# A one-core decoder block: borders of phases in another order, all splits on VectorE, state space steps further apart, and pre-norm gains in the weights' rows

## The chip, the cores and the metric

The kernel runs on one core of a Trainium2 chip, as one launch. The metric is the device time of that launch in microseconds (us). TensorE does the matrix products, ScalarE (ACT in the profile), VectorE (DVE) and GpSimd (POOL) work beside it, and SyncE (SP) issues most of the loads.

## The reference

256 tokens of 2048 channels, float32 throughout, run through five blocks, each with its norms, and a closing gate:

```python
def first_block(x, ...):                     # two layers
    h = x
    for layer in range(2):
        u = rms_norm(h, mix_norm_pre[layer])
        u = even_mixer(u, ...) if layer == 0 else odd_mixer(u, ...)
        h = h + rms_norm(u, mix_norm_post[layer])
        u = swiglu(rms_norm(h, ffn_norm_pre[layer]), w_gate, w_up, w_down)
        h = h + rms_norm(u, ffn_norm_post[layer])
    return h

def second_block(x, p, ...):
    hn = rmsnorm(h, norm_gain[i]); proj = hn @ w_in[i]
    ya = pool_mixer(...) * silu(pool_gate)
    yb = ssm_mixer(...) * silu(ssm_gate)     # a complex diagonal state space, 64 groups of 16 channels
    h = h + concatenate([ya, yb]) @ w_out[i]
    h = h + (p[i] @ w_ple[i]) * sigmoid(h @ w_ple_gate[i])
    return rmsnorm(h, final_gain)
```

The even mixer is stick-breaking attention and a gated delta rule, the odd one is block attention and dilated attention. A norm is `x * rsqrt(mean(x*x) + eps) * gain`; the gain of a pre-norm is one number per channel, so it may multiply either the normed activations or the rows of the matrix behind them.

## The kernel before

**Units and parts.** Every product with a large matrix is cut into units: 128 rows of the matrix by 512 columns. For float32 accuracy each operand is split in a high and a low piece (`uh`, `ul` of the activations, `wh`, `wl` of the weights), and a unit is three matmuls for each of the two token tiles (t = 0, 1, of 128 tokens): `wh`·`uh` (L300), `wl`·`uh` (L301), `wh`·`ul` (L302). Two units share one chunk of 512 KB, loaded by SyncE into a `wr` tile (L213, five buffers). `split()` (L219) makes a part of a chunk: ScalarE copies `wr` to `wh` (L227), VectorE subtracts to `wl` (L228). Parts are split SA = 3 ahead of the unit at hand, loads run LA = 4 chunks ahead. There are four own buffers for `wh` and `wl`; up to EXTRA more parts may stand in general tiles while `lead[0]` is set, and then GpSimd takes every other subtraction.

**Phases and borders.** The program has the phases mix0, ffn0, mix1, ffn1, blk2 and a last one (`ple` gate and final norm). `order()` (L234) lays out each phase's units: the first 12 (head) run for t=0 and then again for t=1, the middle ones for both, the last 8 (tail) for t=0 and then t=1. So the chain between two phases, in which a token tile's sum of squares, its root, the update of `h`, the transposes of `h` and the split into `uh` and `ul` follow each other, can run for one token tile while TensorE works for the other. Hooks in `order()` say ahead of which unit a step is emitted: T(t, c) transposes four blocks of `h` of tile t, columns 512c and on (L351), and evacuates them to `uh` (ScalarE, L358) and `ul` (VectorE, L360), with the pre-norm gain `gT` as the scale; U(t, c) is `upd` (L415), the update of `h` (VectorE L419 for c < 3; for c = 3 ScalarE L421 and GpSimd L422). T(t, c) has the activations of units 4c to 4c+3. After the last panel of a phase, `post_end` (L409) computes the root (GpSimd, L318).

**Tasks.** Attention, delta rule and state space are generators that `tick()` steps once per unit; `yield n` lets n units pass. `ssm_prep` (L1016) makes the tables of the state space during ffn0: its loop has 16 turns, each of which computes `cpo` (VectorE, L1244), sends it off and multiplies it on TensorE (L1249). `ssm_states` (L1356), in blk2, loads `csn`, multiplies the windows (L1371), has the result evacuated to `vt` by ScalarE (L1375 to L1379), transposes `vt` (L448), runs VectorE's scans into `vw` (L1389), and multiplies by `swap` (L1394).

All engines run their instructions in the order of emission; the program is scheduled by hand, and no planner moves anything.

## Time and profile before

| | |
|---|---|
| median of the three runs | 2908.78 us (2908.42 to 2912.8) |
| the profiled execution | 2910.4 us |
| its span | 2908.4 us |
| TensorE busy | 2826.9 us, 97% |
| VectorE / ScalarE / GpSimd busy | 58% / 47% / 9% |
| mean granted TensorE clock | 0.994 |

The span is the time from the first to the last instruction in the trace. TensorE's busy time is nearly all of it, so the views worth reading are those that say where it was not busy: the list of waits, and the timeline around them. PEclk is the share of full clock that TensorE was granted in a stretch.

### The profile page before, as it was taken

What the parts mean: (1) busy time and instruction counts of PE and PEld (TensorE: products, weight loads), DVE (VectorE), ACT (ScalarE), POOL (GpSimd) and SP (SyncE); (2) the same over time, 40 slices, a digit from 0 to 9 for tenths busy, and PEclk for the clock granted to TensorE, in tenths of its full rate; (3) what the DMA queues carried; (4) which work ended last, traced back from release to release, by engine and by line L of the source; (5) the groups of instructions that cost most, each with busy time, mean ns of one, the idle gap of its engine ahead of it and who ended that gap; (6) DMA issues with size and microseconds to landing.
All of it is one profiled execution on the core that took longest, in us unless ns stands there. A gap on an engine that the chain in (4) does not pass through costs nothing. (4 is left out here: it accounts for less than half of the span.)

```text
span 2908.4 us, 35734 instructions
## 1 busy us (share of the span) xinstructions
PE 2826.9 (97%) x13503; PEld 2314.7 (80%) x13503; DVE 1676.7 (58%) x2170; ACT 1357.4 (47%) x1876; POOL 258.1 (9%) x316
## 2 busy tenths in 40 slices
PE   8999999999999999989999999999999999999998
PEld 6877778778888778877888878888888887778887
DVE  5675555677665665565555564544544556464555
ACT  5554454544444434445444454444444445444444
POOL 1141510100000111020000010000000002100010
PEclk9999999999999999999999999999999999999999
DMA  7664645576767667645556656666666665875554
GB/s 229 179 166 126 179 151 175 165 200 201 221 210 214 202 201 252 202 153 173 172 167 181 189 164 189 188 192 192 188 190 194 189 200 167 290 232 179 188 192 153
DMA packets 303613, 552.17 MB, mean 190 GB/s; under 512 B 43032, under 2 KB 48720, under 8 KB 303440
## 3 DMA queue, kind: packets, MB, share of 16 engines
q1 hardware_dynamic: 293216, 515.53, 58.5%
q0 software_dynamic: 10224, 34.35, 3.7%
q8 instruction: 106, 1.74, 0.2%
q14 instruction: 67, 0.55, 0.1%
HBM read 532.24 MB, written 21.76 MB: 190 GB/s over the span
## 5 line engine op out<-in xcount | busy, mean ns | idle before, releaser
L228 DVE TENSOR_TENSOR wl<-wr,wh 128x1024 fp32r<-128x1024 f32 x930 | 1144.4, 1233 | 1040.7 <-ACT wh L227 1037.7
L227 ACT ACTIVATE wh<-wr 128x1024 fp32r<-128x1024 f32 x948 | 1000.5, 1059 | 1053.0 <-PE mm L302 1000.7
L300 PE MATMUL mm<-wh,uh 128*128 128x512 f32 x2624 | 1055.2, 402 | 2.9 <-ACT wh L227 2.2
L302 PE MATMUL mm<-wh,ul 128*128 128x512 f32 x2624 | 1028.4, 392 | 11.6 <-DVE ul L360 11.6
L301 PE MATMUL mm<-wl,uh 128*128 128x512 f32 x2624 | 1026.4, 391 | 4.3 <-DVE wl L228 4.3
L302 PEld LDWEIGHTS mm<-wh,ul 128*128 128x128 f32 x2624 | 494.2, 188 | 122.1 <-DVE ul L360 17.0
L300 PEld LDWEIGHTS mm<-wh,uh 128*128 128x128 f32 x2624 | 495.5, 189 | 104.5 <-ACT wh L227 4.2
L301 PEld LDWEIGHTS mm<-wl,uh 128*128 128x128 f32 x2624 | 495.8, 189 | 102.7 <-DVE wl L228 7.3
L300 PE MATMUL mm<-wh,mh 128*128 128x512 f32 x832 | 327.4, 394 | 0.0
L302 PE MATMUL mm<-wh,ml 128*128 128x512 f32 x832 | 324.5, 390 | 0.0
L301 PE MATMUL mm<-wl,mh 128*128 128x512 f32 x832 | 324.4, 390 | 0.0
L300 PEld LDWEIGHTS mm<-wh,mh 128*128 128x128 f32 x832 | 156.5, 188 | 33.4 <-issue 2.0
L302 PEld LDWEIGHTS mm<-wh,ml 128*128 128x128 f32 x832 | 156.5, 188 | 32.9
L301 PEld LDWEIGHTS mm<-wl,mh 128*128 128x128 f32 x832 | 156.6, 188 | 31.4
L485 POOL TENSOR_TENSOR acc<-acc,wpost 128x512 f32<-128x512 f32 x12 | 15.3, 1296 | 833.9 <-ACT junk L322 833.9
L358 ACT ACTIVATE uh<-aux,gT 128x128 fp32r<-128x128 f32 x160 | 45.5, 367 | 46.9 <-PE aux L351 46.9
L228 POOL TENSOR_TENSOR wl<-wr,wh 128x1024 fp32r<-128x1024 f32 x18 | 46.2, 2576 | 217.4 <-ACT wh L227 217.4
L360 DVE SCALAR_TENSOR_TENSOR ul<-aux,gT,uh 128x128 fp32r<-128x128 f32 x160 | 44.9, 342 | 33.1 <-ACT uh L358 33.1
L331 ACT ACTIVATE mh<-aux 128x512 fp32r<-128x512 f32 (+1 forms) x60 | 32.4, 540 | 66.2 <-PE aux L448 44.5
L332 DVE TENSOR_TENSOR ml<-aux,mh 128x512 fp32r<-128x512 f32 (+1 forms) x60 | 37.1, 619 | 31.1 <-ACT mh L331 28.7
L318 POOL TENSOR_TENSOR rp<-ms,half 128x1 f32<-128x1 f32 x8 | 10.2, 1273 | 476.9 <-DVE ms L317 476.9
L419 DVE SCALAR_TENSOR_TENSOR h<-acc,rp,h 128x512 f32<-128x512 f32 x24 | 44.6, 1884 | 1.8 <-POOL rp L318 1.8
(447 smaller groups left out, 2053.2 us busy)
## 6 DMA issues: line engine op xcount, KB each, us to landing
wr<-in_ffn_w_gate_dram SPq DMA_DIRECT2D x176, 512.0 KB, 4.2
wr<-in_ffn_w_up_dram SPq DMA_DIRECT2D x176, 512.0 KB, 3.8
wr<-in_ffn_w_down_dram SPq DMA_DIRECT2D x176, 512.0 KB, 4.6
wr<-in_ev_w_in_dram SPq DMA_DIRECT2D x112, 512.0 KB, 3.8
wr<-in_od_w_in_dram SPq DMA_DIRECT2D x96, 512.0 KB, 3.7
...
```

The costliest lines, as they stand in the source:

```text
L227: ACT.activation(hi, r[:, k:k + m, :], AF.Copy)
L228: (POOL if lead[0] and ns[0] % 2 else DVE).tensor_sub(lo, r[:, k:k + m, :], hi.bitcast(F32))
L300: PE.matmul(o, a, wh, start=u["first"], stop=False)
L301: PE.matmul(o, a, wl, start=False, stop=False)
L302: PE.matmul(o, b, wh, start=False, stop=u["last"])
L318: POOL.tensor_tensor(r[:, t:t + 1], m, half[:, 0:1], OP.pow)
L331: ACT.activation(hi, src, AF.Copy)
L332: DVE.tensor_sub(lo, src, hi.bitcast(F32))
L358: ACT.activation(self.hi[:, 4 * c + i, ts], p4[:, i * P:(i + 1) * P], AF.Copy, scale=g[i])
L360: DVE.scalar_tensor_tensor(self.lo[:, 4 * c + i, ts], p4[:, i * P:(i + 1) * P], g[i], self.hi[:, 4 * c + i, ts].bitcast(F32), OP.mult, OP. ...
L419: DVE.scalar_tensor_tensor(h[:, t, sl], a, rp[:, t:t + 1], h[:, t, sl], OP.mult, OP.add)
L485: (DVE if j == 3 else POOL).tensor_mul(acc, acc, cut(st["wpost"], j))
```

## The change

Four things change together.

1. The pre-norm gain moves from the activations to the weights. `gemm` takes `gi`, and `split()` of a chunk with a gain makes each half of 128x512 apart: ScalarE scales a row by `gT`, VectorE computes row times `gT` minus `wh` in one scalar_tensor_tensor. That holds for the 624 chunks that are multiplied with `uh` in mix0, the two ffn's gate and up matrices, mix1 and blk2's `w_in`; the others are split whole, as before. T() loses the gain: one ACTIVATE and one subtraction of 128x512 in place of four and four of 128x128. `ab_proj`, which has weights of its own, gets a multiplication.
2. At the borders, GpSimd splits nothing any more. EXTRA is 3, and `lead` holds for the t=0 halves of head and of tail; in the tail's t=1 half nothing is split (`hold`) but at one unit. The hooks move: T(0,0) one unit later, U(0,2) into the tail, T(0,2) two units earlier, t=1's root and updates later.
3. `upd` is one VectorE instruction for every c, and behind an ffn the last panel's product with `wpost` comes behind the root.
4. `ssm_prep`'s loop lets three units pass instead of one ahead of the matmul, `ssm_states` three instead of one ahead of the transposes of `vt` and four instead of two ahead of the `swap` product.

```diff
-    def gemm(src, wap, kts, panels, evac, kc=2):
+    def gemm(src, wap, kts, panels, evac, kc=2, gi=None):
...
-    LA, SA, HEAD, TAIL, EXTRA, CAP = 4, 3, 12, 8, 2, 3
-    lead = [False]
+    LA, SA, HEAD, TAIL, EXTRA, CAP = 4, 3, 12, 8, 3, 3
+    lead, hold = [0], [False]
...
-            if own == 4 and (not lead[0] or len(live) == 4 + EXTRA):
+            if own == 4 and len(live) >= 4 + lead[0]:
                 return
...
-            ACT.activation(hi, r[:, k:k + m, :], AF.Copy)
-            (POOL if lead[0] and ns[0] % 2 else DVE).tensor_sub(lo, r[:, k:k + m, :], hi.bitcast(F32))
+            if gi is None:
+                ACT.activation(hi, r[:, k:k + m, :], AF.Copy)
+                DVE.tensor_sub(lo, r[:, k:k + m, :], hi.bitcast(F32))
+            else:
+                for i in range(m):
+                    split_evac(hi[:, i, :], lo[:, i, :], r[:, k + i, :], gT[:, gi * KT + kk + i:][:, :1])
...
-            hooks = {0: [U(0, 2)], 1: [T(0, 1)], 2: [U(0, 3)], 3: [U(1, 0), U(1, 1)], 6: [T(0, 2)],
-                     HEAD - 2: [T(1, 0)], HEAD - 1: [T(1, 1)], HEAD - 5: [U(1, 2), U(1, 3)],
+            C = lambda t: (lambda: st["post"](t))
+            hooks = {1: [T(0, 1)], 2: [C(1), U(0, 3)], 4: [T(0, 2)], 6: [U(1, 0), U(1, 1)],
+                     HEAD - 2: [T(1, 0)], HEAD - 1: [T(1, 1)], HEAD - 4: [U(1, 2), U(1, 3)],
...
-                seq.append((u, (t,), hooks.get(i, []), t == 0))
+                seq.append((u, (t,), hooks.get(i, []), EXTRA if t == 0 else 0, False))
...
-                hooks = {TAIL + 2: [U(0, 0), U(0, 1)], 2 * TAIL - 2: [n2.begin, lambda n2=n2: n2.T(0, 0)]}
+                hooks = {TAIL: [C(0)], TAIL + 3: [U(0, 0), U(0, 1)], TAIL + 5: [U(0, 2)],
+                         2 * TAIL - 1: [n2.begin, lambda n2=n2: n2.T(0, 0)]}
...
-                seq.append((u, (t,), hooks.get(i, []), nx is not None and t == 1))
+                seq.append((u, (t,), hooks.get(i, []), EXTRA if nx else 0, nx and t == 1 and i != TAIL + 1))
...
-            split(si + SA + (EXTRA if ts == (1,) else 0))
+            if not hold[0]:
+                split(si + SA + lead[0])
...
-            if self.gi is None:
-                split_evac(self.hi[:, ks, ts], self.lo[:, ks, ts], h4(p4))
-                return
...
+            split_evac(self.hi[:, ks, ts], self.lo[:, ks, ts], h4(p4))
...
-            a = cut(acc[t], c)
-            if c < 3:
-                DVE.scalar_tensor_tensor(h[:, t, sl], a, rp[:, t:t + 1], h[:, t, sl], OP.mult, OP.add)
-            else:
-                ACT.activation(a, a, AF.Copy, scale=rp[:, t:t + 1])
-                POOL.tensor_add(h[:, t, sl], h[:, t, sl], a)
-        st["upd"] = upd
+            DVE.scalar_tensor_tensor(h[:, t, sl], cut(acc[t], c), rp[:, t:t + 1], h[:, t, sl], OP.mult, OP.add)
+        st.update(upd=upd, post=post)
...
+            DVE.tensor_mul(r, r, gT[:, :KT, None].to_broadcast([P, KT, 16]))
...
             DVE.tensor_sub(o[:, :, 1:], o[:, :, 1:], tm)
-            yield 1
+            yield 3
...
-                yield 1
+                yield 3
                 ps = transposes(vt)
...
-                yield
+                yield 4
                 ps = aux()
                 PE.matmul(ps[:, :S], ssm["swap"], v, start=True, stop=True)
```

ScalarE at the border from ffn0 to mix1, before: `junk` is the square sum of the last panel of a token tile (t=0, then t=1), `uh` the evacuations of T(0,0), T(0,1) and T(0,2), `wh` the splits.

```order
L227 ACTIVATE wh<-wr 128x1024 x3
L322 ACTIVATE junk,ssp<-acc 128x512
L227 ACTIVATE wh<-wr 128x1024 x4
L358 ACTIVATE uh<-aux,gT 128x128 x4
L227 ACTIVATE wh<-wr 128x1024
L322 ACTIVATE junk,ssp<-acc 128x512
L358 ACTIVATE uh<-aux,gT 128x128 x4
L421 ACTIVATE acc<-acc,rp 128x512
L227 ACTIVATE wh<-wr 128x1024
L358 ACTIVATE uh<-aux,gT 128x128 x4
```

The same place after, from the last whole parts of the ffn on (L329 is the old L322, L338 the old L358, L341 the split with a gain):

```order
L228 ACTIVATE wh<-wr 128x1024 x3
L341 ACTIVATE wh<-wr,gT 128x512 x6
L329 ACTIVATE junk,ssp<-acc 128x512
L338 ACTIVATE uh<-aux 128x4x128
L329 ACTIVATE junk,ssp<-acc 128x512
L341 ACTIVATE wh<-wr,gT 128x512 x8
L338 ACTIVATE uh<-aux 128x4x128 x6
```

One whole part stood between the first and the second `uh` before, beside the square sum; now eight scaled halves, four parts, stand there, and none behind it until T(0,2) and the later ones are out.

VectorE at the same border, before: `acc` is the last panel's sum and `wpost` product, `ms` the mean for the root, `h` the updates, `ul` the low pieces of T(0,0), T(0,1) and T(0,2).

```order
L228 TENSOR_TENSOR wl<-wr,wh 128x1024
L419 SCALAR_TENSOR_TENSOR h<-acc,rp,h 128x512 x2
L228 TENSOR_TENSOR wl<-wr,wh 128x1024
L360 SCALAR_TENSOR_TENSOR ul<-aux,gT,uh 128x128 x4
L228 TENSOR_TENSOR wl<-wr,wh 128x1024
L482 TENSOR_TENSOR acc<-mm,acc 128x512
L485 TENSOR_TENSOR acc<-acc,wpost 128x512
L316 TENSOR_REDUCE ms<-ssp 128x1
L317 TENSOR_SCALAR ms<-ms 128x1
L419 SCALAR_TENSOR_TENSOR h<-acc,rp,h 128x512
L360 SCALAR_TENSOR_TENSOR ul<-aux,gT,uh 128x128 x4
L419 SCALAR_TENSOR_TENSOR h<-acc,rp,h 128x512 x2
L360 SCALAR_TENSOR_TENSOR ul<-aux,gT,uh 128x128 x4
```

And after (L339 is the old L360, L342 the split with a gain, L415 the late `wpost` product, L479 the old L482, L323 and L324 the old L316 and L317):

```order
L324 TENSOR_SCALAR ms<-ms 128x1
L415 TENSOR_TENSOR acc<-acc,wpost 128x512
L419 SCALAR_TENSOR_TENSOR h<-acc,rp,h 128x512 x3
L339 TENSOR_TENSOR ul<-aux,uh 128x4x128
L479 TENSOR_TENSOR acc<-mm,acc 128x512
L342 SCALAR_TENSOR_TENSOR wl<-wr,gT,wh 128x512 x8
L339 TENSOR_TENSOR ul<-aux,uh 128x4x128
L323 TENSOR_REDUCE ms<-ssp 128x1
L324 TENSOR_SCALAR ms<-ms 128x1
L415 TENSOR_TENSOR acc<-acc,wpost 128x512
L419 SCALAR_TENSOR_TENSOR h<-acc,rp,h 128x512
L339 TENSOR_TENSOR ul<-aux,uh 128x4x128
```

Three updates stand ahead of the first `ul` instead of two, and eight halves of `wl` between the first and the second; the root's inputs for t=1 come behind the second.

VectorE in a turn of the state space's preparation, before: `cpo` is what the matmul of L1249 reads, `kr` is made from that matmul's result, one unit later; `wl` are the splits.

```order
L1244 TENSOR_TENSOR cpo<-cpo,cpt 128x4x128
L228 TENSOR_TENSOR wl<-wr,wh 128x1024
L1254 SCALAR_TENSOR_TENSOR kr<-dd,kr 128x16
L228 TENSOR_TENSOR wl<-wr,wh 128x1024 x2
L1239 TENSOR_TENSOR cpo<-pw,c_7550 128x4x128
L1241 TENSOR_TENSOR cpt<-pw,c_7551 128x512
L1244 TENSOR_TENSOR cpo<-cpo,cpt 128x4x128
```

And after, where L1243 is the old L1244 and L1253 the old L1254:

```order
L1243 TENSOR_TENSOR cpo<-cpo,cpt 128x4x128
L342 SCALAR_TENSOR_TENSOR wl<-wr,gT,wh 128x512 x4
L1253 SCALAR_TENSOR_TENSOR kr<-dd,kr 128x16
L342 SCALAR_TENSOR_TENSOR wl<-wr,gT,wh 128x512 x4
L1238 TENSOR_TENSOR cpo<-pw,c_7893 128x4x128
L1240 TENSOR_TENSOR cpt<-pw,c_7894 128x512
L1243 TENSOR_TENSOR cpo<-cpo,cpt 128x4x128
```

One part's subtraction lay between `cpo` and `kr`; now the four halves of two parts do, and the turn is longer by one part.

## Rows read from the trace of the kernel before

**Rows 1.** The page's part 1, whole span: busy us (share) x instructions

```profile
PE 2826.9 (97%) x13503; PEld 2314.7 (80%) x13503; DVE 1676.7 (58%) x2170; ACT 1357.4 (47%) x1876; POOL 258.1 (9%) x316
```

**Rows 2.** TensorE's waits, whole span: line <- releaser, us, times, longest us

```profile
PE mm L302 <- DVE ul L360: 11.6, 10, 1.6
PE aux L351 <- DVE h L419: 10.7, 4, 3.1
PE aux L1249 <- DVE cpo L1244: 8.2, 16, 1.4
PE aux L886 <- ACT X L879: 4.6, 1, 4.6
PE aux L448 <- ACT vt L1375: 4.4, 1, 4.4
PE mm L301 <- DVE wl L228: 4.3, 6, 0.8
...
PE aux L1394 <- DVE vw L1389: 2.8, 3, 1.0
...
PE mm L300 <- ACT wh L227: 2.2, 1, 2.2
...
PE aux L448 <- DVE tmq L513: 1.4, 1, 1.4
```

**Rows 3.** Timeline, border ffn0 to mix1: start, us, engine, instruction, [idle before]

```profile
1276.59 0.69 DVE L482 TENSOR_TENSOR acc<-mm,acc 128x512 f32<-128x512 f32 x1 [3.12 <-PE mm L302]
...
1278.01 3.88 ACT L227 ACTIVATE wh<-wr 128x1024 fp32r<-128x1024 f32 x4
...
1279.16 1.57 POOL L318 TENSOR_TENSOR rp<-ms,half 128x1 f32<-128x1 f32 x1 [9.86 <-DVE ms L317]
...
1280.71 5.14 POOL L228 TENSOR_TENSOR wl<-wr,wh 128x1024 fp32r<-128x1024 f32 x2
1280.76 5.63 DVE L419 SCALAR_TENSOR_TENSOR h<-acc,rp,h 128x512 f32<-128x512 f32 x2 [0.45 <-POOL rp L318]
...
1283.74 0.63 PE L351 MATMUL aux<-ident,h 128*128 128x128 f32 x4 [3.11 <-DVE h L419]
...
1292.01 0.74 DVE L419 SCALAR_TENSOR_TENSOR h<-acc,rp,h 128x512 f32<-128x512 f32 x1
```

**Rows 4.** Windows: stretch, us, busy us of each engine, PEclk, DMA share, GB/s

```profile
1268.00:1280.00 12.00, 12.00 (x54) 9.95 (x53) 6.85 (x8) 5.12 (x8) 2.14 (x3) 1.00 0.44 143
...
510.60:514.00 3.40, 3.40 (x11) 2.44 (x8) 3.40 (x3) 2.50 (x6) 1.67 (x1) 0.50 0.50 151
...
1284.10:1288.00 3.90, 2.28 (x12) 1.58 (x11) 3.90 (x5) 2.09 (x5) 1.75 (x1) 1.00 0.48 134
...
2425.50:2432.30 6.80, 5.88 (x18) 4.83 (x19) 6.80 (x9) 2.09 (x5) 3.00 (x2) 0.50 0.44 132
```

**Rows 5.** Groups by form, whole span: xcount | busy, mean ns | idle before

```profile
L464 DVE SCALAR_TENSOR_TENSOR mid<-mm,rs,sg 128x512 f32<-128x512 f32 x44 | 30.8, 742 | 0.0
...
L421 ACT ACTIVATE acc<-acc,rp 128x512 f32<-128x512 f32 x8 | 5.9, 736 | 0.0
...
L332 DVE TENSOR_TENSOR ul<-aux,uh 128x512 fp32r<-128x512 f32 x8 | 5.5, 688 | 10.3 <-ACT uh L331 10.3
```

**Rows 6.** The page's part 5, the splits of whole parts

```profile
L228 DVE TENSOR_TENSOR wl<-wr,wh 128x1024 fp32r<-128x1024 f32 x930 | 1144.4, 1233 | 1040.7 <-ACT wh L227 1037.7
L227 ACT ACTIVATE wh<-wr 128x1024 fp32r<-128x1024 f32 x948 | 1000.5, 1059 | 1053.0 <-PE mm L302 1000.7
```

**Rows 7.** Timeline, one turn of the state space's preparation

```profile
959.91 0.68 DVE L1244 TENSOR_TENSOR cpo<-cpo,cpt 128x512 f32<-128x512 f32 x1
...
960.74 0.43 PE L1249 MATMUL aux<-cpo,bb 128*32 128x128 f32 x8 [1.10 <-DVE cpo L1244]
```

**Rows 8.** Timeline, SyncE and ScalarE ahead of the first scan of the states

```profile
2501.52 16.36 SPq L1318 DMA_DIRECT2D ur<-ud  x16
...
2522.25 1.06 ACT L227 ACTIVATE wh<-wr 128x1024 fp32r<-128x1024 f32 x1 [7.44 <-DMA wr<-in_w_in_dram]
```

More of the change, by code (lines that the diff above doesn't have):

```diff
@@ L162, in trunk, with phase @@
     phs = []
-    def phase(gi=None, norm=True, begin=None):
-        phs.append(dict(a=len(units), gi=gi, norm=norm, begin=begin))
-    def gemm(src, wap, kts, panels, evac, kc=2):
+    def phase(norm=True, begin=None):
+        phs.append(dict(a=len(units), norm=norm, begin=begin))
+    def gemm(src, wap, kts, panels, evac, kc=2, gi=None):
         for j, (c0, c1) in enumerate(panels):
@@ L172, in gemm @@
                 ks = kts[g:g + kc]
-                chunks.append((wap, ks, c0, c1))
+                chunks.append((wap, ks, c0, c1, gi))
                 for i, k in enumerate(ks):
@@ L207, in fetch @@
             ci = nf[0]
-            wap, ks, c0, c1 = chunks[ci]
+            wap, ks, c0, c1, gi = chunks[ci]
             n, kc = c1 - c0, len(ks)
@@ L215, in fetch @@
             for k in range(0, kc, step):
-                parts.append((ci, k, min(step, kc - k), n, r))
+                parts.append((ci, k, min(step, kc - k), n, r, gi, ks[k]))
             nf[0] += 1
@@ L276, in run_units @@
             pass
-        for u, ts, hooks, lead[0] in order():
+        for u, ts, hooks, lead[0], hold[0] in order():
             for f in hooks:
@@ L352, in T @@
             ks, ts = slice(4 * c, 4 * c + 4), slice(t * P, (t + 1) * P)
-            if self.gi is None:
-                split_evac(self.hi[:, ks, ts], self.lo[:, ks, ts], h4(p4))
-                return
-            g = [gT[:, self.gi * KT + 4 * c + i:][:, :1] for i in range(4)]
-            for i in range(4):
-                ACT.activation(self.hi[:, 4 * c + i, ts], p4[:, i * P:(i + 1) * P], AF.Copy, scale=g[i])
-            for i in range(4):
-                DVE.scalar_tensor_tensor(self.lo[:, 4 * c + i, ts], p4[:, i * P:(i + 1) * P], g[i],
-                                         self.hi[:, 4 * c + i, ts].bitcast(F32), OP.mult, OP.subtract)
+            split_evac(self.hi[:, ks, ts], self.lo[:, ks, ts], h4(p4))
         def stats(self):
-            st["upd"] = lambda t, c: None
+            st.update(upd=lambda t, c: None, post=lambda t: None)
             if self.norm:
@@ L405, in post_evac, with post_end, post @@
         DVE.tensor_mul(cut(st["acc"][t], j), src, cut(st["wpost"], j))
-        if j == 3:
-            post_end(t)
-    def post_end(t):
-        if t == 0:
-            st["rp"] = small("rp")
-        rstd_of(st["ssp"], t, st["rp"])
-        acc, rp = st["acc"], st["rp"]
+        if j == 3 and t == 0:
+            post_end(False)
+    def post_end(late):
+        acc, ssp, wpost, rp = st["acc"], st["ssp"], st["wpost"], small("rp")
+        def post(t):
+            rstd_of(ssp, t, rp)
+            if late:
+                DVE.tensor_mul(cut(acc[t], 3), cut(acc[t], 3), cut(wpost, 3))
         def upd(t, c):
             sl = slice(c * 512, (c + 1) * 512)
-            a = cut(acc[t], c)
-            if c < 3:
-                DVE.scalar_tensor_tensor(h[:, t, sl], a, rp[:, t:t + 1], h[:, t, sl], OP.mult, OP.add)
-            else:
-                ACT.activation(a, a, AF.Copy, scale=rp[:, t:t + 1])
-                POOL.tensor_add(h[:, t, sl], h[:, t, sl], a)
-        st["upd"] = upd
+            DVE.scalar_tensor_tensor(h[:, t, sl], cut(acc[t], c), rp[:, t:t + 1], h[:, t, sl], OP.mult, OP.add)
+        st.update(upd=upd, post=post)
     def cols(n, base=0, w=512):
@@ L451, in ffn @@
     def ffn(layer, gi, begin=None, end=None):
-        phase(gi, begin=begin)
+        phase(begin=begin)
         wg, wu, wd = I["ffn_w_gate"][layer], I["ffn_w_up"][layer], I["ffn_w_down"][layer]
@@ L570, in begin @@
             st["masks"] = (m[:, :3 * P], m[:, 3 * P:])
-        phase(2, begin=begin)
+        phase(begin=begin)
         for g in range(4):
@@ L966, in sb_head @@
             split_evac(mh[:, 4 * g + i, :], ml[:, 4 * g + i, :], po[:, :S])
-        phase(0, begin=begin)
+        phase(begin=begin)
         def tm(T, n):
@@ L1555, in ple_evac @@
             return f
-        phase(None, norm=False)
+        phase(norm=False)
         for j in range(4):
```

35 lines of the change are left out of this document (18 added, 17 removed).

## The prediction

> **What bounds the kernel now.** I read the busy shares first [rows 1]: TensorE is busy 2826.9 of 2908.4 us, VectorE 58% and ScalarE 47%. So only time in which TensorE stands still, or runs at its lower clock, can be won, and a longer split of weights costs nothing as long as the parts stay ahead of TensorE. Next comes the table of what TensorE waited for [rows 2]. Its largest entries are the places that the diff touches: 11.6 us for `ul`, 10.7 us for `h`, 8.2 us for `cpo` in the state space's preparation, 4.4 us for `vt`, 4.3 us for `wl`, 2.8 us for the scans' `vw`. Then the timeline of one border between phases [rows 3]: GpSimd takes 1.57 us for the root, then splits two parts in 5.14 us; beside it two `h` updates on VectorE take 5.63 us, where one alone takes 0.74. TensorE, at T(0,0), waits 3.11 us for the first of them. [...]
>
> The profiled execution took 2910.4 us for a span of 2908.4; the median of the three runs is 2908.78, so I take 1.6 us off at the end.
>
> **Splitting with the weight inside.** A part of 128x1024 now takes one ACTIVATE of 1.06 us and one VectorE instruction of 1.23 us [rows 6]. In the 624 chunks read from `uh` it becomes two and two of 128x512. The nearest rows are the scaled `acc` (0.736 us, an ACTIVATE of 128x512 with a scale per partition, as the new `wh` half) and the gated product (0.742 us, a scalar_tensor_tensor of that size, as the new `wl` half) [rows 5]. So at most 1.47 us on ScalarE and 1.48 us on VectorE for each part, 0.41 and 0.25 us more. TensorE needs 12 matmuls for a part: 54 started in 12.00 us [rows 4], 0.22 us each, so 2.7 us. Both engines stay at 55% of that plus their other work; in the middle of a phase I cost the change at nothing, hidden by parts that are split three ahead. The cover is thin where chains of small steps share the two queues (delta rule, attention): their steps find a longer instruction ahead of them. The largest wait there is 4.6 us, for the delta rule's X [rows 2], the others are shorter: I take +2, between 0 (nothing shows) and +5 (such a wait again).
>
> [...]
>
> **The borders.** What goes: GpSimd's splits (two in 5.14 us here), so updates on VectorE take 0.74 us each; the four and four small instructions for `uh` and `ul` of each T become one and one, as the last phase has them already (`ul` 0.688 us [rows 5]); T(0,0) comes one unit later. Before, the waits for `h` and `ul` are 10.7 + 11.6 = 22.3 us [rows 2]. In the two stretches at 0.50 TensorE was busy for 3.40 and 5.88 us [rows 4], which full clock would halve, 4.6 us; part of that lies beside waits that are counted already, so I add 3: 25.3 us.
>
> What comes: tail's t=1 half splits no part but one (the new `hold`), and the backlog is split when head starts. The order of instructions shows it: between `uh` of T(0,0) and of T(0,1) ScalarE now has a square sum and eight scaled halves, where one `wh` stood; VectorE has eight halves between the two `ul`. TensorE needs T(0,1) in unit 4, and has only two groups of transposes (0.63 us each [rows 3]) and four units of one token tile (three matmuls, 0.68 us each), then two matmuls: 4.4 us from the last unit of the phase to the first use of `ul`(0,1). VectorE arrives there by this chain behind an ffn phase, worked out for t=1 from the rows of t=0: last sum to first `wh` 1.42 us (1276.59 to 1278.01 [rows 3]), the first half on ScalarE 0.74, eight on VectorE 5.9, `ul` 0.69: 8.8 us. Wait: 4.4 us. Behind a mixer there is no sum ahead of the squares, 0.7 less: 3.7 us. Instructions in a row overlap: four `wh` took 3.88 us [rows 3], 4.24 by their mean. With that I take 4.0 and 3.3, between 2.4 (a fifth less for the eight, and the square sum earlier) and 4.4. T(0,0) itself: from the last sum of t=0 to the root's start 2.57 us, the root 1.57, one update 0.74, 4.9 us; seven units are 4.8: no wait. `ul`(0,0) is due 1.7 us behind T(0,0)'s start and ready after two instructions of 0.6 to 0.7 behind transposes of 0.63, 1.9: with the clock's edges 0.5. Two borders of each kind: 2 x (4.0 + 0.5) + 2 x (3.3 + 0.5) = 16.6 us. Stops of 3 us are on both sides of what lowered the clock before, so I add 4 us (0 to 6.4: none to four stretches of 1.6, half of 3.4 less a little). Sum 20.6 against 25.3: **-5**, between -15 and 0.
>
> At the border to the last phase nothing is scaled, but four whole parts now stand ahead of T(0,1): 0.7 + 1.06 + 4 x 1.23 + 0.69 = 7.4 us against 4.4, 3.0; with overlap 2.5, where the trace of before has no row of a wait over 0.5: **+2** (+1 to +3). At the start, T(0,1) stands behind ten scaled halves and SyncE issues x behind more `wr`; `ab_proj` has one multiplication more: **+1** (0 to +2.5).
>
> Behind each border TensorE waits for `wl` and once for `tmq` (4.3 and 1.4 us [rows 2]). The backlog is split earlier and the whole first half of head runs six parts ahead: I take **-3**, half of the two (-5 to 0).
>
> **The steps of the state space.** In the preparation's 16 turns `cpo` is ready at most 1.4 us late [rows 2], since it stands behind a `wl` on VectorE (the turn at 960 us: L1244 starts at 959.91, TensorE waited 1.10 us [rows 7]). Two units more are 2.7 us: all 16 waits go, **-8** (-10, since a stop costs TensorE a little more than the wait listed, to -6). The turn is two units longer, so the loop ends 32 units later, still within the ffn phase's middle; its GpSimd transfers meet nothing there. In the states, three units instead of one (2.7 us more) lie between the window products and the transposes of `vt`, and four instead of two ahead of the swap product. The 2.8 us for `vw` go [rows 2]. The 4.4 us for `vt` were really a want of weights: SyncE spent 16.36 us on sixteen `ur` loads, and ScalarE, with `vt` in its queue, waited 7.44 us for `wr` [rows 8]. TensorE will walk on for two units more and may then want weights itself: I take half back, 2.2 us, and 1 of slow matmuls behind so long a stop: **-6**, between -10 and -2. The chain ends 14 units later; its drain stands 44 units behind that.
>
> **Sum.** +2 - 5 + 2 + 1 - 3 - 8 - 6 = -17: 2910.4 - 17 = 2893.4 for a profiled run, 2892 for the median.
>
> **The rivals.**
> - *The backlog does not bind* (the splits run while TensorE is still in the tail): for it, ScalarE is half idle; against it, the first square sum of t=1 stands ahead of the eight halves in its queue and waits for the phase's last matmul. All border waits would go: 2892 - 20.6 - 2.5 = 2869. Chance 0.10.
> - *The new gaps move waits instead of ending them*: the preparation's `cpo` and the states find other work in the queues, as two splits of 1.48 us fit into two units. Then the 8 and 6 us stay: 2892 + 14 = 2906, no difference that counts. Against it: a wait of at most 1.4 us meets 2.7 us. Chance 0.12.
> - *The lower clock at all four borders and longer*: as at 2425 us, where 6.8 us ran at half the clock [rows 4]. Each border then loses about 3 us (half of 5.88), 12 in place of 4: 2900. Against it: the 3.11 us wait at 1280 us left the clock at 1.00. Chance 0.11. [...]
> - *Longer splits starve the mixers* (the slower side): in the 208 chunks of ev_w_in and od_w_in, whose queues also carry attention and delta rule. If each lost 0.15 us (of the 0.41 more on ScalarE), that is 31 us in place of the 2 above: 2890 + 31 = 2921. It decides from 0.12 us per chunk on. Against it: in the whole program TensorE waited for `wh` once, 2.2 us [rows 2]. Chance 0.05.
>
> **How the numbers follow.** My forecast has 0.62: within 2878 to 2903 by its bounds. 2892 is its time. The range 2874 to 2904 holds it, the clock's case and the nearer part of two others, some 0.8. A measurement of this kernel tells 0.2% from no change, 5.8 us: faster is below 2903.0. Faster: 0.62 + 0.10 + 0.11 = 0.83; the same: 0.12; slower: 0.05.
>
> **What would show it.** Right: in the waits, no L1248 behind `cpo`; no `vw`; waits of 3 to 4.5 us of L307 or L309 for `uh`/`ul` some 3 us into each head, with eight scaled halves ahead of them in ScalarE's and VectorE's timeline; updates of `h` at 0.74 us; halves of `wl` near 0.74 us. Wrong: borders without a wait; many new waits for `wh` or `wl` in the mixers; L445 behind `vt` still at 4 us.

## The result and the profile after

The changed kernel takes 2878.35 us (median of four, 2876.55 to 2881.85) beside 2908.6 us for the kernel before: a ratio of 0.9895, with the 95% interval 0.9878 to 0.9912. That is 30 us faster where I had forecast 17. The direction and the range held; the size was too small by almost half, and the time lies at the edge of the 2878 to 2903 us that I gave my own forecast. The profiled execution's span went from 2908.4 to 2875.6 us.

The page's part 1 of the kernel after, whole span, which answers to [rows 1]:

```profile
PE 2825.3 (98%) x13503; PEld 2314.6 (80%) x13503; DVE 1772.4 (62%) x2701; ACT 1502.0 (52%) x2374; POOL 193.1 (7%) x290
```

TensorE is as busy as before, to 1.6 us. VectorE and ScalarE work 96 and 145 us more, and none of that shows in the time: 31.2 of the span's 32.8 us are time in which TensorE stood still.

TensorE's waits after, answering to [rows 2] (line, releaser, us in total, times, longest):

```profile
PE mm L307 <- ACT uh L338: 12.7, 5, 3.3
PE aux L445 <- DVE mid L461: 3.6, 2, 3.3
...
PE mm L309 <- DVE ul L339: 2.0, 2, 1.5
...
PE aux L885 <- ACT X L878: 1.7, 1, 1.7
PE mm L309 <- DVE ms L323: 1.5, 3, 0.5
...
PE mm L307 <- ACT wh L341: 1.3, 1, 1.3
...
PE mm L308 <- DVE wl L342: 0.2, 1, 0.2
```

Gone are the waits for `cpo`, `vt`, `vw`, `tmq` ahead of L448 and the `h` of the borders, and 4.1 of the 4.3 us for `wl`. What is new is the wait for `uh`: two of 3.3 us, two of 2.0 and, at the start of the program, one of 1.9. The three waits of 0.5 put down to `ms` are waits for `ul`(0,1) behind them; the list names another VectorE instruction.

The same border as in [rows 3], after; timeline, from the updates of t=0 to the low piece of T(0,1) (start, us, engine, instruction, [idle before]):

```profile
1267.35 2.08 DVE L419 SCALAR_TENSOR_TENSOR h<-acc,rp,h 128x512 f32<-128x512 f32 x3 [0.45 <-POOL rp L325]
...
1268.25 0.63 PE L358 MATMUL aux<-ident,h 128*128 128x128 f32 x4
...
1270.15 0.68 DVE L479 TENSOR_TENSOR acc<-mm,acc 128x512 f32<-128x512 f32 x1
...
1271.56 5.00 ACT L341 ACTIVATE wh<-wr,gT 128x512 fp32r<-128x512 f32 x8
...
1272.30 5.39 DVE L342 SCALAR_TENSOR_TENSOR wl<-wr,gT,wh 128x512 fp32r<-128x512 f32 x8 [1.47 <-ACT wh L341]
...
1276.46 1.05 ACT L338 ACTIVATE uh<-aux 128x512 fp32r<-128x512 f32 x2
...
1277.09 0.50 PE L307 MATMUL mm<-wh,uh 128*128 128x512 f32 x1 [3.34 <-ACT uh L338]
...
1277.60 0.69 DVE L339 TENSOR_TENSOR ul<-aux,uh 128x512 fp32r<-128x512 f32 x1
...
1278.34 0.50 PE L309 MATMUL mm<-wh,ul 128*128 128x512 f32 x1 [0.52 <-DVE ul L339]
```

T(0,0) starts without a wait, since three updates take 2.08 us where two took 5.63 beside GpSimd's splits. Then the eight scaled halves stand between ScalarE and `uh`(0,1), and between VectorE and `ul`(0,1), and TensorE stands 3.34 + 0.52 = 3.86 us.

The granted clock behind the four inner borders after, answering to [rows 4] (stretch, us, busy us of each engine with instructions, PEclk, DMA share, GB/s):

```profile
514.00:518.00 4.00, 4.00 (x11) 3.14 (x12) 3.97 (x8) 0.00 (x0) 0.99 (x1) 0.57 0.85 313
...
1278.00:1283.00 5.00, 4.66 (x13) 3.69 (x14) 4.97 (x10) 0.00 (x0) 0.93 (x1) 0.66 0.96 326
...
1673.00:1678.40 5.40, 4.88 (x14) 3.53 (x14) 5.07 (x10) 0.17 (x1) 0.98 (x1) 0.68 0.77 267
...
2412.00:2417.40 5.40, 4.93 (x16) 3.79 (x16) 5.37 (x11) 0.00 (x0) 0.92 (x1) 0.68 0.80 280
```

All four have a stretch at half clock: it was 0.50 in every half microsecond from 514.5 to 517.5, 1279.0 to 1282.0, 1675.0 to 1678.0 and 2412.5 to 2415.0 us, where the units' matmuls start 0.43 us apart, and 0.23 us apart at 1.00. In each about 1.7 us of TensorE's time is lost (5.40 x 0.32).

Both kernels run the same 11,376 matmuls of the units in the same order. So the start of one and the same matmul can be compared between the two traces, and the change of its lag from one place to the next says what a stretch gained or lost:

| stretch | change, us | forecast |
|---|---|---|
| start and first mixer units | +0.8 | +1 |
| mixers and middles of the ffn: delta rule's X some -4.5, a wait for `mid` near 605 us +2.4, small ones some +0.9 | -1.2 | +2 |
| inner borders: -2.7 and -2.6 behind the mixers, -5.3 and -0.4 behind ffn0, -2.8 and -2.0 behind ffn1 | -15.8 | -5 and -3 |
| state space's preparation | -9.9 | -8 |
| its states, to the end of blk2's first product | -9.4 | -6 |
| last border | +2.6 | +2 |
| sum | -32.9 | -17 |

### The profile page after: what moved, and what is told of

It is laid out like the page before. It is cut to its first block, busy times and chain, and to the rows that moved or that the text cites. A ratio compares the mean times of both kernels' runs of the same rounds, so it can differ in the third digit from the quotient of the medians.

```text
span 2875.6 us, 36743 instructions
## 1 busy us (share of the span) xinstructions
PE 2825.3 (98%) x13503; PEld 2314.6 (80%) x13503; DVE 1772.4 (62%) x2701; ACT 1502.0 (52%) x2374; POOL 193.1 (7%) x290
## 4 chain that ended last, share of the span: by engine, by line
PE 91%; DVE 3%; DMA 2%; ACT 1%; POOL 1%; issue 1%; SPq 0%; ACTq 0%; POOLq 0%; DVEq 0%
PE mm L307 28%; PE mm L309 28%; PE mm L308 28%; DVE wl L342 2%; PE aux L445 1%; ACT wh L341 1%; PE aux L358 1%; POOL xb L870 1%; POOL rk L868 0%; PE aux L1333 0%; DMA h<-in_x_dram 0%; PE aux L560 0%; DMA wr<-in_ffn_w_up_dram 0%; DMA b<-in_b_im_dram 0%; DMA wr<-in_ev_w_in_dram 0%
## 5 line engine op out<-in xcount | busy, mean ns | idle before, releaser
L342 DVE SCALAR_TENSOR_TENSOR wl<-wr,gT,wh 128x512 fp32r<-128x512 f32 x1248 | 881.0, 750 | 558.9 <-ACT wh L341 557.7
L341 ACT ACTIVATE wh<-wr,gT 128x512 fp32r<-128x512 f32 x1248 | 828.3, 715 | 533.0 <-PE mm L309 493.6
L307 PE MATMUL mm<-wh,uh 128*128 128x512 f32 x2624 | 1057.0, 403 | 14.1 <-ACT uh L338 12.7
L309 PE MATMUL mm<-wh,ul 128*128 128x512 f32 x2624 | 1029.8, 392 | 3.5 <-DVE ul L339 2.0
L229 DVE TENSOR_TENSOR wl<-wr,wh 128x1024 fp32r<-128x1024 f32 x324 | 401.6, 1244 | 360.8 <-ACT wh L228 360.1
L307 PEld LDWEIGHTS mm<-wh,uh 128*128 128x128 f32 x2624 | 496.0, 189 | 118.8 <-ACT uh L338 16.4
L309 PEld LDWEIGHTS mm<-wh,ul 128*128 128x128 f32 x2624 | 495.3, 189 | 114.3 <-DVE ul L339 7.4
L228 ACT ACTIVATE wh<-wr 128x1024 fp32r<-128x1024 f32 x324 | 342.3, 1059 | 399.9 <-PE mm L309 392.9
L307 PE MATMUL mm<-wh,mh 128*128 128x512 f32 x832 | 326.5, 392 | 0.0
L309 PE MATMUL mm<-wh,ml 128*128 128x512 f32 x832 | 324.0, 389 | 0.0
L309 PEld LDWEIGHTS mm<-wh,ml 128*128 128x128 f32 x832 | 156.2, 188 | 32.8
L307 PEld LDWEIGHTS mm<-wh,mh 128*128 128x128 f32 x832 | 156.2, 188 | 32.8 <-issue 1.2
L338 ACT ACTIVATE uh<-aux 128x512 fp32r<-128x512 f32 x48 | 28.0, 591 | 84.6 <-PE aux L358 84.6
L339 DVE TENSOR_TENSOR ul<-aux,uh 128x512 fp32r<-128x512 f32 x48 | 33.0, 690 | 57.6 <-ACT uh L338 57.4
L338 ACT ACTIVATE mh<-aux 128x512 fp32r<-128x512 f32 (+1 forms) x60 | 32.4, 539 | 62.5 <-PE aux L445 42.8
L339 DVE TENSOR_TENSOR ml<-aux,mh 128x512 fp32r<-128x512 f32 (+1 forms) x60 | 37.1, 619 | 33.3 <-ACT mh L338 32.6
```

Of the source, the lines that this page charges most:

```text
L228: ACT.activation(hi, r[:, k:k + m, :], AF.Copy)
L229: DVE.tensor_sub(lo, r[:, k:k + m, :], hi.bitcast(F32))
L307: PE.matmul(o, a, wh, start=u["first"], stop=False)
L309: PE.matmul(o, b, wh, start=False, stop=u["last"])
L338: ACT.activation(hi, src, AF.Copy)
L339: DVE.tensor_sub(lo, src, hi.bitcast(F32))
```

## The experiments

Each was timed beside the kernel before on the same chip; that stood at 2907.3 to 2909.0 us. Edits are shown against the kernel after, unless another is named.

**The steps of the state space, undone.** First the gaps alone, back at their old lengths:

```diff
-            yield 3
+            yield 1
...
-                yield 3
+                yield 1
...
-                yield 4
+                yield
```

> The changed kernel with the three gaps of the state space as before (one unit ahead of the preparation's matmul, one ahead of the transposes of vt, two ahead of the swap product). Theory (the gaps hid waits that the queues make in any case): the 16 waits for cpo come back with 8 to 11 us, those of the states with 8 to 10: 2893 to 2899 us. Rival (VectorE's shorter instructions have already ended the waits, the gaps add nothing): 2877 to 2883 us.

It took 2895.68 us (2890.69 to 2898.94), 17 above the kernel after by the medians and 14 by the spans. Its waits are the old ones, that for `cpo` a little shorter (7.2 us where it was 8.2), that for `vt` by almost half:

```profile
PE aux L1248 <- DVE cpo L1243: 7.2, 16, 1.4
...
PE aux L445 <- ACT vt L1374: 2.5, 1, 2.5
```

All 16 turns wait for `cpo` again.

**The same from the other side.** The kernel before, with only the three gaps made longer (the edit above turned round):

> The kernel before with the three larger gaps of the state space alone. Theory (the gaps are worth the same with or without the rest, as undoing them in the changed kernel cost 14 to 17 us): 14 to 20 us under the kernel before, 2888 to 2894 us; no wait for cpo and none for vw. Rival (the gaps need the shorter instructions beside them): 8 us and less, 2900 to 2904 us.

2890.41 us (2888.84 to 2893.19), ratio 0.9944 (0.9929 to 0.9958): 16.9 faster by the medians and 19.4 by the spans: -9.9 in the preparation and -9.2 in the states by the starts of the same matmuls, much as in the kernel after (-9.9 and -9.4). From either side the gaps are worth 17 us by the medians, so nothing shows that they hang on the rest of the change. I had forecast 14.

**The gain back in T.** `wh` and `wl` of whole parts, T() with four and four scaled instructions of 128x128; hooks, hold and gaps stay as after:

```diff
-            if gi is None:
-                ACT.activation(hi, r[:, k:k + m, :], AF.Copy)
-                DVE.tensor_sub(lo, r[:, k:k + m, :], hi.bitcast(F32))
-            else:
-                for i in range(m):
-                    split_evac(hi[:, i, :], lo[:, i, :], r[:, k + i, :], gT[:, gi * KT + kk + i:][:, :1])
+            ACT.activation(hi, r[:, k:k + m, :], AF.Copy)
+            DVE.tensor_sub(lo, r[:, k:k + m, :], hi.bitcast(F32))
...
+            for i in range(4):
+                ACT.activation(self.hi[:, 4 * c + i, ts], p4[:, i * P:(i + 1) * P], AF.Copy, scale=g[i])
+            for i in range(4):
+                DVE.scalar_tensor_tensor(self.lo[:, 4 * c + i, ts], p4[:, i * P:(i + 1) * P], g[i],
+                                         self.hi[:, 4 * c + i, ts].bitcast(F32), OP.mult, OP.subtract)
```

> The changed kernel with the pre-norm gain back in T() (four and four small instructions), and all parts split whole, one instruction on ScalarE and one on VectorE; borders and gaps stay as changed. Theory (GpSimd gets through sooner beside VectorE's short instructions, and that is why the delta rule's X came sooner): the wait for X at 352 us, now 1.7 us, is back at 4 to 5 us; at the borders the backlog is 1 us shorter and T 1 us longer, so they stay within 1 us each; 2880 to 2886 us. Rival (X came sooner for another reason, such as the order at the start): X waits 1.7 us, 2875 to 2880 us.

2882.58 us (2879.74 to 2885.68), ratio 0.9915 (0.9901 to 0.993): the gain in the weights is worth 4 us by the medians and 3 by the spans; the intervals of the two ratios overlap, so the places have to bear it out. The gains of the inner borders change by 1 to 2 us each, 1.1 in all. There are two larger differences, of opposite sign: in mix0 the wait for the delta rule's X is back at 3.7 us and the lag grows by some 3.5, and near 605 us the wait for `mid` is back at the 1.7 us of the kernel before and the lag falls by 2.9. The waits of this run (line, releaser, us in total, times, longest):

```profile
PE aux L888 <- ACT X L881: 3.7, 1, 3.7
...
PE aux L449 <- DVE mid L465: 1.7, 1, 1.7
```

Both go with the splits in every run here. With whole parts (this kernel, the kernel before, the kernel before with the gaps alone, and the one with GpSimd splitting again) X waits 3.7 to 4.6 us and `mid` at most 1.7; with scaled halves X waits at most 2.7, and `mid` 3.3 in all seven kernels that load `b` by SyncE. For `mid` the timeline says why: behind weights that come late, VectorE has several parts in a row to split ahead of it, and a part of two halves takes it 1.41 us where a whole one takes 1.22.

In the prediction the longer splits cost at X, if anything. The rows say why they gain there. GpSimd computes the inverse of the delta rule in 62 small products, one behind the other, and X waits for their end. The groups of those products (line, operation, names, shapes, count, busy us, mean ns, idle before), first in the kernel before:

```profile
L871 POOL TENSOR_TENSOR xb<-xb,rk 128x60 f32<-128x60 f32 (+24 forms) x31 | 15.7, 506 | 2.4
L869 POOL TENSOR_TENSOR rk<-mb,xb 128x60 f32<-128x60 f32 (+24 forms) x31 | 14.4, 466 | 10.1 <-DMA mb<-ms 7.7
```

and in the kernel after:

```profile
L870 POOL TENSOR_TENSOR xb<-xb,rk 128x60 f32<-128x60 f32 (+24 forms) x31 | 14.1, 455 | 2.4
L868 POOL TENSOR_TENSOR rk<-mb,xb 128x60 f32<-128x60 f32 (+24 forms) x31 | 13.1, 423 | 9.5 <-DMA mb<-ms 7.2
```

30.1 us became 27.2, with the same products: 2.9 of some 4.5 us. The rest lies in the steps around them and was not followed up. One of them in the kernel before, with what VectorE did at the time (timeline; a product that meets no work of VectorE takes 0.2 to 0.34 us):

```profile
339.00 1.23 DVE L228 TENSOR_TENSOR wl<-wr,wh 128x1024 fp32r<-128x1024 f32 x1 [1.40 <-ACT wh L227]
```

```profile
339.06 1.27 POOL L871 TENSOR_TENSOR xb<-xb,rk 128x24 f32<-128x24 f32 x1
```

The product at 339.06 ends at 340.33, VectorE's subtraction at 340.23. Thirteen of the 62 products took over 0.7 us, and each of them ended 0.1 to 0.2 us behind a subtraction of VectorE. Beside halves of 0.75 us the longest of the 62 in the kernel after took 0.83. So a product here waits for about the rest of the instruction that it meets.

**Halves without the gain.** If the length of VectorE's instruction is the cause, halves must do the same in the kernel before, with the gain left where it was. Against the kernel before:

```diff
-            (POOL if lead[0] and ns[0] % 2 else DVE).tensor_sub(lo, r[:, k:k + m, :], hi.bitcast(F32))
+            if lead[0] and ns[0] % 2:
+                POOL.tensor_sub(lo, r[:, k:k + m, :], hi.bitcast(F32))
+            else:
+                for i in range(m):
+                    DVE.tensor_sub(lo[:, i, :], r[:, k + i, :], hi[:, i, :].bitcast(F32))
```

> The kernel before with one thing changed: VectorE subtracts each part in two halves of 128x512 instead of one instruction of 128x1024; gain, borders and gaps as before. Theory (GpSimd's instructions wait for the end of the VectorE instruction beside them, and shorter ones let the delta rule's inverse through): the wait for X at 352 us falls from 4.6 to some 2 us, the time to 2903 to 2907 us. Rival: X still waits 4.6 us and the time stays at 2907 to 2911 us.

2906.59 us (2900.84 to 2910.89), ratio 0.9998 (0.9989 to 1.0007): no change that can be told by the medians (the profiled spans differ by 3.8 us). The mechanism is there: the products take 27.1 us (L875 and L873 below), the wait for X falls from 4.6 to 0.7 us, and the lag there by 5.35. But it is given back elsewhere, as the waits show:

```profile
L875 POOL TENSOR_TENSOR xb<-xb,rk 128x60 f32<-128x60 f32 (+24 forms) x31 | 14.0, 453 | 2.4
L873 POOL TENSOR_TENSOR rk<-mb,xb 128x60 f32<-128x60 f32 (+24 forms) x31 | 13.1, 422 | 9.4 <-DMA mb<-ms 7.0
```

```profile
PE aux L1253 <- DVE cpo L1248: 9.9, 16, 1.5
...
PE aux L452 <- DVE mid L468: 3.4, 2, 2.6
...
PE aux L452 <- DVE tmq L517: 2.2, 1, 2.2
```

`cpo` waits 1.7 us more than in [rows 2], `mid` 1.3 (2.1 before) and `tmq` 0.8. In the kernel after, the longer gaps cover the first of these. That this is why halves paid there and not here is my reading; the wait for `mid` grew there too, as above, and the one for `tmq` was not followed up.

**GpSimd splitting again.** The kernel with the gain in T, and every other subtraction of the runs ahead given back to GpSimd:

```diff
-            DVE.tensor_sub(lo, r[:, k:k + m, :], hi.bitcast(F32))
+            (POOL if lead[0] and ns[0] % 2 else DVE).tensor_sub(lo, r[:, k:k + m, :], hi.bitcast(F32))
```

> The kernel with the gain back in T() and whole parts (2882.6 us), and with GpSimd taking every other subtraction in the t=0 halves of head and tail again. Theory (GpSimd's splits, which slow VectorE beside them, cost the borders of the kernel before their waits for h): updates of h or parts beside them take 2 us and more, 2 to 4 us at each border, 2890 to 2898 us. Rival (in the new order GpSimd's splits meet no update and shorten the backlog, since two engines share it): 2874 to 2881 us.

2900.0 us (2898.01 to 2902.01): 17.4 more than without GpSimd, a little beyond the range that I had expected. The border from ffn0 to mix1 (timeline):

```profile
1279.30 5.65 POOL L228 TENSOR_TENSOR wl<-wr,wh 128x1024 fp32r<-128x1024 f32 x2 [6.34 <-ACT wh L227]
1280.20 5.83 DVE L228 TENSOR_TENSOR wl<-wr,wh 128x1024 fp32r<-128x1024 f32 x2 [2.74 <-ACT wh L227]
...
1286.35 0.80 PE L305 MATMUL mm<-wh,ul 128*128 128x512 f32 x1 [3.15 <-DVE ul L363]
```

Two parts on each engine take 5.7 us; four on VectorE alone take 4.9 by its 1.23 us of [rows 6]. A part that meets no work of VectorE takes GpSimd 2.4 us (2.39 at 2788 us in the kernel before). Helping makes both slower, and `ul` waits behind it.

The four changes now have their prices, step by step in medians: gaps 2907.3 to 2890.4; the new order at the borders with GpSimd still splitting, 2900.0 (9.6 worse); GpSimd out, 2882.6; gain in the weights, 2878.35. The starts of the same matmuls say where. At the four inner borders the new order with GpSimd splitting gains 0.5 us in all, GpSimd out 14.2 and the gain in the weights 1.1, together the 15.8 of the table; the new order with GpSimd splitting loses 6.2 at the last border and 1.7 at the start and in mix0. So in the new order the borders gain because GpSimd no longer splits; taking it out in the old order was not tried.

**T(0,1) earlier.** By my reading the eight halves ahead of `uh`(0,1) hold TensorE. Here T(0,1) is emitted at the first unit of head, ahead of the backlog:

```diff
-            hooks = {1: [T(0, 1)], 2: [C(1), U(0, 3)], 4: [T(0, 2)], 6: [U(1, 0), U(1, 1)],
+            hooks = {0: [T(0, 1)], 2: [C(1), U(0, 3)], 4: [T(0, 2)], 6: [U(1, 0), U(1, 1)],
...
+                hooks[1] = [T(0, 1)]
```

> The changed kernel with one step moved: T(0,1) is emitted ahead of unit 0 of each head instead of unit 1, so its two evacuations stand ahead of the eight halves (four parts) that are split at the head's start. Theory (the backlog in the queues is what TensorE waits for at the borders): the waits for uh behind unit 3, 3.3 us behind an ffn and about 2 us behind a mixer, go, the one at the last border (1.5 us) too; T(0,2) now stands behind the backlog, so a wait of 0 to 1.5 us appears ahead of unit 8; with the slow clock behind the stops gone the time is 8 to 14 us under the changed kernel: 2864 to 2871 us. Rival (the chain of transposes, uh and ul itself is too long, wherever it stands): the same waits come back at unit 8, 2876 to 2881 us.

2868.32 us (2866.91 to 2871.86), ratio 0.9868 (0.9853 to 0.9883): 10 better than the kernel after by the medians, 5.5 by the spans; the intervals of the ratios just overlap. Both mixers' borders gain 2.8 us each, the start and the last border together 1.9, the borders behind the ffn only 0.75 and 0.45; mix0 lost 3.5, and no view here shows why. Behind the ffn the wait goes on to T(0,2), at unit 8 (timeline, ffn0 to mix1):

```profile
1278.21 0.50 PE L308 MATMUL mm<-wh,uh 128*128 128x512 f32 x1 [1.53 <-ACT uh L339]
...
1280.99 0.50 PE L310 MATMUL mm<-wh,ul 128*128 128x512 f32 x1 [2.04 <-DVE ul L340]
```

**T(0,1) and T(0,2) earlier.** Both ahead of the backlog, at units 0 and 1, which is split from unit 1 on:

```diff
+            hooks = {0: [T(0, 1)], 1: [T(0, 2)], 2: [C(1), U(0, 3)], 6: [U(1, 0), U(1, 1)],
...
+                seq.append((u, (t,), hooks.get(i, []), EXTRA if t == 0 else 0, pi > 0 and t == 0 and i == 0))
```

> The changed kernel with T(0,1) ahead of unit 0 and T(0,2) ahead of unit 1 of each head, and the backlog of four parts split only from unit 1 on, behind them. Theory (TensorE waits for whatever evacuation stands behind the backlog; with T(0,1) alone moved the wait went to T(0,2), 1.5 and 2.0 us at the border from ffn0): no wait of more than 0.6 us at T(0,1) or T(0,2), no stretch at half the clock behind the four borders, 15 to 22 us under the changed kernel: 2856 to 2864 us. Rival (the backlog then comes too late, and TensorE waits for wh or wl of it instead): new waits of 1 to 3 us for L341 or L342 in each head, 2866 to 2874 us.

2871.68 us (2869.58 to 2872.49), short of what I had expected and no better than T(0,1) alone. The wait goes on again, now to t=1: its root's inputs and updates stand behind the eight halves on VectorE (timeline, same border):

```profile
1271.60 5.38 DVE L344 SCALAR_TENSOR_TENSOR wl<-wr,gT,wh 128x512 fp32r<-128x512 f32 x8
...
1277.76 3.40 DVE L421 SCALAR_TENSOR_TENSOR h<-acc,rp,h 128x512 f32<-128x512 f32 x5
...
1279.31 0.63 PE L360 MATMUL aux<-ident,h 128*128 128x128 f32 x4 [3.70 <-DVE h L421]
```

**Without the hold.** Parts are split all through the tail, so no backlog stands at head:

```diff
-            if not hold[0]:
-                split(si + SA + lead[0])
+            split(si + SA + lead[0])
```

> The changed kernel without the hold: parts go on being split during the tail's t=1 half, as buffers come free. Theory (the hold makes the backlog, and the backlog is the wait): the waits at unit 4, 3.9 us behind an ffn and 2.5 behind a mixer, fall under 1.5 us, the updates of h wait at most one part: 2866 to 2874 us. Rival (the hold pays for itself, since it keeps VectorE free for the updates of h): T(0,0) waits 2 to 4 us for h at each border, 2876 to 2886 us.

2870.8 us (2867.62 to 2876.88), 7.5 better than the kernel after by the medians and 9.8 by the spans, though the intervals of the ratios, 0.9865 to 0.9899 here, overlap. The waits at unit 4 are gone, as I had expected, but a split stands ahead of `ul`(0,0) instead, one part and not four, and TensorE waits there:

```profile
1266.78 1.41 DVE L341 SCALAR_TENSOR_TENSOR wl<-wr,gT,wh 128x512 fp32r<-128x512 f32 x2
...
1268.84 0.51 PE L308 MATMUL mm<-wh,ul 128*128 128x512 f32 x1 [2.44 <-DVE ul L338]
```

So the hold, as it stands in the change, shows no gain, and seems to lose.

**One part a unit.** In the first two of the last three runs four parts stand in a row, in the third a part stands within the chain. Here no unit of the halves for one token tile splits more than one part, the hold is cut to the three units ahead of T(0,0), and T(0,1) comes at unit 0:

```diff
+            if one[0]:
+                return
...
+            hooks = {0: [T(0, 1)], 2: [C(1), U(0, 3)], 4: [T(0, 2)], 6: [U(1, 0), U(1, 1)],
...
+                seq.append((u, (t,), hooks.get(i, []), EXTRA if nx else 0, nx and t == 1 and TAIL + 4 <= i < 2 * TAIL - 1))
...
+            one[0] = len(ts) == 1
```

> The changed kernel with the backlog spread: in the single-tile halves of head and tail at most one part is split in a unit, the hold lasts only from the tail's fifth to its seventh unit of t=1 (from the updates of h to T(0,0)), and T(0,1) stands ahead of unit 0. Theory (VectorE is the bound of the border, since updates, ul and the backlog's halves share it; a part costs least where none of the chain's steps stands behind it): waits for uh, ul and h of at most 1 us each at the four borders, none of 2 us, little time at half the clock; 2858 to 2866 us. Rival (the sum of VectorE's work between the tail's t=1 half and unit 12 is too long, wherever the parts stand): 2868 to 2872 us, as with the three other ways of moving the backlog.

2858.22 us (2856.9 to 2860.24), ratio 0.9827 (0.9812 to 0.9842): 20 better than the kernel after by the medians, 17 by the spans, and the lowest of all. Every border gains over the kernel after: 2.5 to 4.4 us each of the inner ones, 2.6 the last and 2.75 the start. The wait behind ffn0, longer than the 1 us that I had expected, and the clock around it:

```profile
1274.79 0.50 PE L313 MATMUL mm<-wh,ul 128*128 128x512 f32 x1 [1.72 <-DVE ul L343]
```

```profile
1264.00:1280.00 16.00, 14.03 (x70) 10.76 (x71) 13.19 (x22) 7.16 (x13) 0.93 (x1) 1.00 0.53 160
```

The clock stays at 1.00 in this stretch, and likewise at the other three borders (508 to 520, 1660 to 1672 and 2396 to 2404 us), so the 6.9 us of the slow stretches are saved with the waits. The run makes three edits at once; what each is worth was not separated, but T(0,1) at unit 0 alone gave 5.5 to 10 us and no hold alone 7.5 to 9.8.

**T(0,1) in the tail on top of it**, and T(0,2) at unit 1:

```diff
+            hooks = {1: [T(0, 2)], 2: [C(1), U(0, 3)], 6: [U(1, 0), U(1, 1)],
...
+                         2 * TAIL - 1: [n2.begin, lambda n2=n2: n2.T(0, 0), lambda n2=n2: n2.T(0, 1)]}
```

> As the spread backlog with one step more: T(0,1) stands with T(0,0) ahead of the tail's last unit, so that its uh is not behind the last square sum, and T(0,2) ahead of unit 1. Theory: what is left of the waits for uh and ul at the start of the heads goes too, 2 to 5 us under the spread backlog alone: 2855 to 2863 us. Rival (the wait then goes to T(1,0), as where the backlog came behind both transposes, 3.7 us for h): no gain on the spread backlog.

2859.97 us (2859.08 to 2863.19): no gain. The waits for `ul`, 4.5 us at the four borders, went to T(1,0), which waits 6.6 us for `h` there. By my reading the remaining chain is that of t=1's root.

**The loads of `b` by another queue.** The largest wait left, 3.3 us for `mid` in ffn0, stands behind weights that come late while `ssm_prep` loads its four `b` arrays. Against the kernel with one part a unit, these loads are issued by GpSimd:

```diff
-                nc.sync.dma_start(o[64 * i:64 * i + 64].rearrange("n (g c) -> n g c", c=16),
+                POOL.dma_start(o[64 * i:64 * i + 64].rearrange("n (g c) -> n g c", c=16),
```

> The kernel with the spread backlog (2858.2 us), and the state space's four b loads, of small rows, issued by GpSimd instead of SyncE. Theory (in the changed kernel the wait of 3.3 us for mid at 605 us comes from weights that stand behind those loads in SyncE's queue: ScalarE waited 7.75 us for wr there): the wait for mid falls under 1 us, ScalarE's wait for wr goes, 3 to 5 us less, 2853 to 2856 us. Rival (the small rows take the transfer engines, whoever issues them): mid still waits 2 us and more, 2857 to 2860 us.

2859.05 us (2857.62 to 2863.03): no change, and the theory of SyncE's queue fell. GpSimd issues these loads from 529 us on, SyncE from 569 us, and the stop moved with them, from 604 to 557 us. The weights are nearly as late (7.0 us where it was 7.9), and TensorE waits no less (timeline and window):

```profile
545.71 1.34 ACT L345 ACTIVATE wh<-wr,gT 128x512 fp32r<-128x512 f32 x2 [7.03 <-DMA wr<-in_ffn_w_up_dram]
...
556.92 1.11 PE L449 MATMUL aux<-ident,mid 128*128 128x128 f32 x4 [4.66 <-DVE mid L465]
```

```profile
530.00:556.00 26.00, 22.27 (x99) 18.11 (x97) 11.76 (x18) 13.05 (x20) 5.76 (x4) 0.98 1.02 205
```

The transfer engines are full (DMA share 1.02) while the clock of TensorE is not the matter (0.98). In the kernel after, where SyncE issues them, the share is 1.06 from 574 to 592 us. So they are full while these rows of 16 numbers are loaded, whoever issues. Smaller pieces spread over more time, or another layout of `b`, were not tried.

## Why the prediction was right, and where it was short

**Direction and mechanism held.** What I listed as signs came: no wait for `cpo` or `vw`, updates of `h` at full speed (three in 2.08 us), waits of L307 and L309 at each head with eight scaled halves ahead of them. The halves are in the page's part 5 (count, busy us, mean ns):

```profile
L342 DVE SCALAR_TENSOR_TENSOR wl<-wr,gT,wh 128x512 fp32r<-128x512 f32 x1248 | 881.0, 750 | 558.9 <-ACT wh L341 557.7
L341 ACT ACTIVATE wh<-wr,gT 128x512 fp32r<-128x512 f32 x1248 | 828.3, 715 | 533.0 <-PE mm L309 493.6
```

They take 750 and 715 ns, where I took 742 and 736 from [rows 5].

**The backlog: right in kind, the sum in part by luck.** Behind the ffn I worked out a chain of 8.8 us, and it was 8.1 (1270.15 to 1278.29). For T(0,1) I took waits of 4.0 us behind an ffn and 3.3 behind a mixer; they were 3.86 and 2.04 + 0.53 = 2.57. The 0.5 for `ul`(0,0) did not come. Eight halves in a row take 5.39 us, 0.67 us each, not 5.9. With the clock (6.9 us, where I took 4 and bounded at 6.4) the new cost is 19.7 us against 20.6. That the two are so near is luck: the waits were shorter than I took and the stretches of lower clock longer.

**Borders: the step that failed is the credit.** -8 was forecast with `wl`, -15.8 measured. I had summed the old borders as 25.3 us: each wait for `h` and `ul` as the list has it, 22.3, and 3 for the clock. From the start of the matmul ahead to the start of the one behind, less the 0.23 us that lie between two matmuls without a stop, the fifteen waits there (one of them for `uh`, which I had left out) cost 25.3 us by themselves, and the two slow stretches all of their 4.6: 29.9. Counted in the same way the new ones cost 13.7 + 6.9 = 20.6, so the borders gain 9.3 where I had 5. Of the `wl` and `tmq` waits I took half, 3 us. Four of the six for `wl` and that for `tmq` lie behind the borders, and all of these went; a stop listed at 0.8 moves the next matmul by 1.0, so they are worth some 5.7. That makes 15.0 of the 15.8.

**Mixers: the wrong sign.** The step "longer splits, +2, hidden or a wait for X again" looked for a cost in queues and at X in the right place; what acts there is that GpSimd's products end 0.1 to 0.2 us behind the VectorE instruction they meet, and shorter instructions help them (0.83 us at the longest beside halves, 1.34 beside whole parts): some -4.5. The two runs with the gain in T and with halves alone show it. It was a gain of the change that I had not looked for, since I costed VectorE's halves only by VectorE's time. The cost that I did look for came elsewhere: near 605 us, in ffn0, `mid` waits 1.6 us longer behind the longer splits, and half clock follows (0.68 from 608 to 613 us, 0.50 from 610 to 613), 2.4 us together with a `wl` wait that went. So the +2 was there, and the gain beside it was missed.

**Preparation and states: right in kind, short in size.** All 16 waits for `cpo` went. From the start of the matmul ahead to that of L1249 the 16 turns took 14.4 us, where the kernel after takes 5.1: 9.3 us and not the 8.2 listed. The stretch gained 9.9, close to my outer bound. In the kernel after (timeline) the `cpo` of the turn that stood in [rows 7] is ready long before its matmul:

```profile
960.10 0.68 DVE L1243 TENSOR_TENSOR cpo<-cpo,cpt 128x512 f32<-128x512 f32 x1
...
963.34 0.43 PE L1248 MATMUL aux<-cpo,bb 128*32 128x128 f32 x8
```

For `vt` I took half, since ScalarE would want weights all the same. It does, but TensorE still had parts (answering to [rows 8]):

```profile
2475.31 16.25 SPq L1317 DMA_DIRECT2D ur<-ud  x16
...
2496.06 2.64 ACT L341 ACTIVATE wh<-wr,gT 128x512 fp32r<-128x512 f32 x4 [7.30 <-DMA wr<-in_w_in_dram]
...
2498.61 0.36 ACT L1374 ACTIVATE vt<-aux 128x256 f32<-128x256 f32 x1
...
2499.02 0.77 PE L445 MATMUL aux<-ident,vt 128*128 128x128 f32 x4
```

ScalarE waits 7.30 us for weights as before, `vt` comes behind four halves, and TensorE has units enough: no wait for `vt`, of which I had credited half, and no slow matmuls behind it, for which I took 1. In the kernel before the clock stood at 0.50 from 2524.6 to 2531.3 us, and TensorE was busy for 4.5 us of that.

**The rivals.** "The gaps only move waits" fell, with both runs on the gaps. "The clock low at all four borders" came half true: low at all four, but 1.7 us each and not 3. "The backlog does not bind" fell at once by the waits. "Longer splits starve the mixers" fell: the wait for `wh` is 1.3 us.
